# A two-level seven-product matmul on one core: a sixth block product by sevens in every second group, small sums on GpSimd, half of C scaled last

## The chip, the cores and the metric

The kernel runs on one core of a Trainium2 chip. The engines are named as in the profile: PE is TensorE (matmuls), DVE is VectorE, ACT is ScalarE, POOL is GpSimd, SP is SyncE, which here only issues DMAs. The metric is the device time of one execution in microseconds (us).

## The reference

```
cs = np.cumsum(x, axis=1)
diff = cs - np.concatenate([zeros, cs[:, :-1, :]], axis=1)
return np.matmul(diff, w).astype(np.float32)
```

x is 8 x 2048 x 2048 and w is 2048 x 2048, both float32. The difference of the running sum is x itself, so what is computed is x @ w, with x seen as 16384 rows of 2048. The kernel computes just that.

## The kernel before

x is cut into 128 row tiles of 128 rows. The first four are multiplied plainly, the next eight by two shorter forms; they are the head. Then come 29 groups of four tiles, g, h = g + 2, k = g + 1 and l = g + 3. Each row of x is divided by its largest magnitude (`weigh` on ACT, `scale_of` on DVE), narrowed to float16 by ACT (`narrow`), and turned by a DMA transpose (`turn`); the factor that undoes the scaling is made by POOL (`unit_of`, one element for each partition).

Each group is a product of two rows of blocks by w, where w is cut in 2 x 2 blocks B11 to B22 of 1024 x 1024. On the outer level seven block products replace eight (P1 to P7). Their left sides are blocks of x or wide sums of them: S1 = A21 + A22, S2 = S1 - A11, S3 = A11 - A21, S4 = A12 - S2 with g or h as row 1 and k or l as row 2. Their right sides are blocks of w or T1 to T4, made once in the head. P6 is S2 x T2 and P7 is S3 x T3.

On the inner level a block product is itself done by seven (`by_seven` and what stands in `plan`): the two tiles g and h (or k and l) are the two rows, and the block of w is cut in quarters of 512 columns by 512 rows. A product by seven has seven quarter products p1 to p7 of 4 matmuls each, 28; a whole one (`whole`, in four pieces for each tile) has 32. Before, P1 to P5 go by seven, P6 and P7 whole: 5 x 28 + 2 x 32 = 204 matmuls a group. The left sides s1 to s4 of the quarter products are small sums of x on DVE (`small_sums`, `total`, 128 x 512), held in four scratch places. Their right sides Q1 to Q4 are quarters of w or differences of them. Those with no room to stay are made again each time in the one buffer `flow` by a fill (`fill_by`): a step named `P2.fp4` fills flow for the quarter product p4 of P2.

Results gather in eight PSUM banks. ACT takes a bank to a tile of C in SBUF with the row's factor (`keep`), DVE adds a bank times the factor to it (`add`); a `merge` adds a copy back into a bank. A finished 128 x 512 tile of C is stored (`put`), and its buffer, one of seven, is free again.

Each engine works its instructions strictly in the order written. That order is the list `ORDER`: names of steps with the number of groups ahead, run through once for each group. Loads of x go through F, a ring in SBUF: three places for the first half of a tile and two for the second (line 101). The narrowed tile lies in its first half's place until both transposes have read it, so a place comes free with the second transpose.

Of the kernel before, what the change touches and what calls it, by code (L numbers as in the profile page):

```python
# [10 lines left out]
def kernel(  # L11
# [6 lines left out]
    nc = tc.nc  # L18
    P = 128
# [112 lines left out]
    def scale_of(t):  # L132
        if t < END:
            m2 = sums_of.pop(t)
            m, s, u = (m2[:, i : i + 1] for i in (2, 3, 4))
            scales[t], unit[t] = s, u
            after(
                "dve",
                lambda: nc.vector.tensor_scalar(m, m2[:, :1], m2[:, 1:2], TINY, ADD, MAX),  # L139
            )  # L140
            after("dve", lambda: nc.vector.reciprocal(s, m))  # L141
            sizes[t] = m

    def unit_of(t):
        if t < END:
            u, m = unit[t], sizes.pop(t)
            after("pool", lambda: nc.gpsimd.tensor_scalar(u, m, uw, None, MUL))  # L147
# [346 lines left out]
    class Inner:  # L494
# [20 lines left out]
        def weights(self):  # L515
            places = dict(
                p1=self.t11, p2=self.t21, p3=self.t22, p4=self.Q4,
                p5=self.Q1, p6=self.Q2, p7=self.Q3,
            )
            return {j: pieces_of(t) for j, t in places.items()}  # L520
# [22 lines left out]
    def total(dst, p, q, op):  # L543
        after("dve", lambda: nc.vector.tensor_tensor(dst.all, p.all, q.all, op))  # L544
# [388 lines left out]

    def fill_by(op, a, b):
        def some():
            x, y = (in_twos(t) for t in (a, b))
            after("dve", lambda: nc.vector.tensor_tensor(in_twos(flow), x, y, op))  # L937

        return some

    sevens = {
# [8 lines left out]
                "p5": fill_by(SUB, quarter_of(1, 1, 1), quarter_of(6, 1, 0)),  # L950
# [5 lines left out]

    class Group:
        def __init__(self, g):
# [27 lines left out]
        def quarter(self, P, j, b, fresh):  # L986
            inner, passes = sevens[P]
            if j in passes:
                self.step(f"{P}.f{j}", passes[j])

            def some():
                to, a = self.bank(b, fresh), self.sums[P][j]
                quarter(
                    to, self.real(a), passed if j in passes else inner.weights()[j], fresh
                )
                if isinstance(a, str):
                    self.drop(a, scratch)

            self.step(f"{P}.{j}", some)

        def small_sums(self, P, a, b, dead, places=()):
# [5 lines left out]
            def one(j, p, q, op):  # L1007
                if isinstance(to[j], str):
                    self.take(to[j], scratch)
                total(self.real(to[j]), self.real(p), self.real(q), op)  # L1010
# [37 lines left out]

        def row(self, c):
            return self.tiles[c[3] if c[1] == "1" else {"g": "k", "h": "l"}[c[3]]]  # L1050

        def keep(self, c, b, let=False):
            def some():
                keep(self.take(c, free), self.at[b], unit[self.row(c)])
                self.close(b, let)

            self.step(f"keep.{c}", some)

        def add(self, c, b, tag, let=False):
            def some():  # L1060
                add(self.at[c], self.at[b], unit[self.row(c)])
                self.close(b, let)

            self.step(f"add.{c}.{tag}", some)

        def put(self, c):
            n = 2 * (c[2] == "2") + int(c[4])
            self.step(f"put.{c}", lambda: put(self.at.pop(c), self.row(c), n))

        def plan(self):  # L1070
            tiles = self.tiles
            half = {}
            for c, t in tiles.items():
# [3 lines left out]
                self.step(f"scale.{c}", scale_of, t)  # L1077
# [74 lines left out]
            self.whole("P7", T3, half["g"][0], half["h"][0], *x)  # L1152
# [43 lines left out]
    put.C12g1+0 turn1.h+1 add.C12h1.q+0 P4.p6+0 P4.p5+0 P1.cg+1 P1.p2+1  # L1196
    add.C12h0.q+0 put.C12h0+0 P1.s1+1 narrow1.k+1 P4.s4+0 P4.p3+0 turn0.k+1
    keep.C21g1+0 P1.s2+1 P1.s4+1 P1.p5+1 add.C22h0.x+0 P1.ct+1 add.C21h1.e+0
    unit.h+1 P1.p6+1 unit.g+1 add.C21g1.q+0 add.C21g0.x+0 weigh0.l+1 P1.s3+1
    weigh1.l+1 turn1.k+1 P2.cv+1 P4.p4+0 add.C21g1.x+0 put.C12h1+0 put.C21g1+0  # L1200
    P1.m1+1 P4.p7+0 P1.fp4+1 put.C21g0+0 load.g+2 P2.s1+1 P2.s2+1 P1.p7+1
    P1.m2+1 P2.s4+1 P2.p1+1 P1.p3+1 keep.C11g1+1 S1.g+1 S2.g+1 P1.p4+1
    keep.C11g0+1 add.C21h1.q+0 scale.l+1 unit.l+1 narrow0.l+1 put.C22h0+0
    put.C21h1+0 P2.p2+1 add.C11g0.v+1 P6g.0+1 P2.fp4+1 P2.p6+1 turn0.l+1
    narrow1.l+1 turn1.l+1 keep.C11h1+1 P6g.1+1 P2.s3+1 add.C11g1.q+1 unit.k+1
    S4.g+1 P2.p5+1 P6g.3+1 keep.C11h0+1 add.C11h1.e+1 P2.p7+1 keep.C21h0+0
    add.C11h1.q+1 P6g.2+1 weigh0.g+2 load.h+2 add.C21h0.x+0 P5.p1+1 P2.p4+1
    S3.g+1 keep.C12g1+1 P2.p3+1 keep.C12g0+1 add.C11h0.q+1 put.C11h0+1 P5.fp5+1
    weigh1.g+2 S1.h+1 P7g.0+1 P5.s1+1 P7g.1+1 scale.g+2 P5.cg+1 P5.s2+1 P5.s4+1
    put.C21h0+0 narrow0.g+2 narrow1.g+2 S2.h+1 P5.s3+1 P5.p2+1 P5.p5+1 P5.ct+1  # L1210
    add.C11g1.e+1 P5.fp4+1 P5.p6+1 P5.m1+1 put.C11g0+1 keep.C22g0+1 weigh0.h+2
    weigh1.h+2 S4.h+1 P3.s1+1 put.C11h1+1 P6h.2+1 P6h.1+1 put.C11g1+1 P3.s2+1
    P6h.3+1 P6h.0+1 keep.C12h1+1 P5.p7+1 P5.m2+1 keep.C22h1+1 S3.h+1 P3.s4+1
    P3.s3+1 P7g.2+1 P7g.3+1 P5.p4+1 add.C22g0.x+1 P3.fp2+1 P5.p3+1 keep.C12h0+1
    add.C12h1.z+1 P7h.0+1 load.k+2 P3.p2+1 scale.h+2 narrow0.h+2 P3.p1+1 P7h.2+1
    put.C22g0+1 turn0.g+2 turn1.g+2 add.C12g0.z+1 weigh0.k+2 add.C12g0.q+1
    put.C12g0+1 P4.fp4+1 keep.C22g1+1 P7h.1+1 P7h.3+1 add.C22g1.x+1 put.C22g1+1
    P3.p3+1 add.C22h1.x+1 P4.s1+1 P4.s3+1 put.C22h1+1 keep.C22h0+1 P3.p6+1
    P3.p4+1 add.C12g1.q+1 add.C12g1.z+1 turn0.h+2 add.C12h0.z+1 weigh1.k+2
    narrow1.h+2 load.l+2 P3.p5+1 scale.k+2 P4.p2+1 P4.p1+1 keep.C21g0+1  # L1220
    keep.C21h1+1 P3.p7+1 narrow0.k+2 P1.p1+2 add.C12g1.e+1 add.C12h1.e+1 P4.s2+1
# [16 lines left out]
    groups = [Group(g) for g in range(PLAIN + 8, END, 4)]  # L1238
    for c in groups[0].tiles:
        for s in ("load", "weigh0", "weigh1", "scale", "unit", "narrow0", "narrow1", "turn0", "turn1"):  # L1240
            del groups[0].do[f"{s}.{c}"]
    del groups[1].do["load.g"]
    before = {"P1.s4": lambda: less(*(half_of(t, 0) for t in (in_1.Q2, in_1.t22, in_1.Q1))), "P5.s3": in_5.third}
    for b in range(-early, len(groups) - late):
        for name, ahead in ORDER:
            i = b + ahead
# [39 lines left out]
```

## Time and profile before

| | |
|---|---|
| median of 3 runs | 1456.42 us (1456.38 to 1456.72) |
| profiled execution, first to last instruction | 1455.0 us (no other time is given for it) |
| granted TensorE clock, mean | 0.999 |
| PE / DVE / ACT / POOL busy | 1441.1 / 1333.3 / 967.5 / 48.6 us |
| DMA | 351.59 MB, mean 242 GB/s |

A row of instruction groups reads: line, engine, operation, out <- in, shapes, count, then busy us and mean ns of one, then the engine's idle time before them and who ended it. A row of the windows reads: the stretch in us, its length, then busy us and number of instructions for PE, PE's weight loads, DVE, ACT and POOL, then clock, DMA share and GB/s. A row of the waits reads: who waited for whom, us in total, times, longest. A row of the order of time reads: start, length, engine, line, operation.

### The profile page before, as it was taken

The numbers are of one execution on the slowest core, as the hardware profiler recorded it, in microseconds if no ns is written. First come the engines' busy times: TensorE is split into PE (matmuls) and PEld (weight loads), VectorE is DVE, ScalarE is ACT, GpSimd is POOL, SyncE is SP. The second block draws the span as 40 slices with busy tenths as digits, with TensorE's granted clock in tenths as the row PEclk, the third lists the DMA queues.
The fourth block names the chain that finished last, engine by engine and source line by source line (L and its number), as shares of the span: only waits on it lengthen the run. The fifth ranks groups of instructions, "written<-read, shape, count | busy, mean of one in ns | idle before, by whom it ended". The sixth has DMA issues, their size and how long they took to land.

```text
span 1455.0 us, 20120 instructions
## 1 busy us (share of the span) xinstructions
PE 1441.1 (99%) x6673; PEld 652.6 (45%) x6679; DVE 1333.3 (92%) x2302; ACT 967.5 (66%) x1446; POOL 48.6 (3%) x136
## 2 busy tenths in 40 slices
PE   8999999999999999999999999999999999999998
PEld 3444444444444444444444444444444444444443
DVE  7998899999999999999999999999999999999998
ACT  5887656676666666667666667766666766666662
POOL 0111000000000000000000000000000000000000
PEclk9999999999999999999999999999999999999999
DMA  9999868898888998878998888998878898888983
GB/s 360 367 240 299 236 171 234 248 246 232 234 237 237 248 253 230 235 236 233 260 241 233 231 228 240 260 238 241 225 235 247 247 233 239 226 244 246 253 203 123
DMA packets 377752, 351.59 MB, mean 242 GB/s; under 512 B 274800, under 2 KB 274800, under 8 KB 377520
## 3 DMA queue, kind: packets, MB, share of 16 engines
q1 hardware_dynamic: 377088, 348.47, 84.9%
q0 software_dynamic: 560, 1.84, 0.3%
q8 instruction: 52, 0.85, 0.2%
q14 instruction: 52, 0.43, 0.1%
HBM read 150.99 MB, written 134.22 MB: 196 GB/s over the span
## 4 chain that ended last, share of the span: by engine, by line
PE 96%; DMA 2%; DVE 1%; issue 0%; ACT 0%; SPq 0%; DVEq 0%; ACTq 0%
PE b L573 61%; PE b L554 32%; PE b L275 2%; DMA W<-in_w_dram 1%; DMA W<-in_x_dram 1%; DVE c L584 1%; ACT wb L259 0%; PE b L400 0%; DVE x L544 0%; SPq L219 0%; DVE b L1030 0%; DVE flow L937 0%; DVE inner L544 0%; DVE W L541 0%; ACT c L581 0%
## 5 line engine op out<-in xcount | busy, mean ns | idle before, releaser
L584 DVE SCALAR_TENSOR_TENSOR c<-b,of,c 128x512 f32<-128x512 f32 x790 | 574.1, 747 | 74.3 <-PE b L573 64.3
L554 PE MATMUL b<-W,x 128*128 128x512 f16 x2144 | 506.6, 379 | 0.0
L581 ACT ACTIVATE c<-b,of 128x512 f32<-128x512 f32 x492 | 312.6, 680 | 230.9 <-PE b L573 113.3
L573 PE MATMUL b<-W,x 128*128 128x512 f16 x1892 | 452.4, 379 | 0.8 <-ACT b L1023 0.7
L158 ACT ACTIVATE F<-F,of 128x1024 f16<-128x1024 f32 x246 | 282.2, 1147 | 174.8 <-DVE of L141 172.6
L573 PEld LDWEIGHTS <-x 128*128 128x128 f16 x2488 | 243.4, 98 | 295.3 <-issue 2.7
L554 PEld LDWEIGHTS <-x 128*128 128x128 f16 x2144 | 209.8, 98 | 253.0 <-DVE x L544 0.2
L123 ACT ACTIVATE waste<-F 128x1024 uint8<-128x1024 f32 x246 | 259.3, 1054 | 4.6 <-DMA F<-in_x_dram 2.5
L573 PEld LDWEIGHTS <-inner 128*128 128x128 f16 x1648 | 161.2, 98 | 195.6 <-issue 1.3
L573 PE MATMUL b<-W,inner 128*128 128x512 f16 x944 | 242.2, 379 | 0.9 <-DVE b L1030 0.9
L544 DVE TENSOR_TENSOR x<-x,x 128x1024 f16<-128x1024 f16 (+1 forms) x388 | 226.6, 584 | 3.3
L573 PE MATMUL b<-flow,x 128*128 128x512 f16 x588 | 150.9, 379 | 0.0
L573 PE MATMUL b<-inner 128*128 128x512 f16 x472 | 121.1, 379 | 0.0
L937 DVE TENSOR_TENSOR flow<-W 128x2048 f16<-128x2048 f16 x87 | 105.8, 1216 | 0.0
L1030 DVE TENSOR_TENSOR b<-b,c 128x512 f32<-128x512 f32 x116 | 80.6, 695 | 13.9 <-PE b L573 13.9
L147 POOL TENSOR_SCALAR of<-of,uw 128x1 f32<-128x1 f32 x124 | 43.6, 370 | 1306.7 <-DVE of L139 704.1
L937 DVE TENSOR_TENSOR flow<-W,inner 128x2048 f16<-128x2048 f16 x58 | 70.8, 1220 | 0.0
L1023 ACT COPY c<-b 128x512 f32<-128x512 f32 x58 | 33.4, 576 | 51.3 <-PE b L573 51.3
L275 PE MATMUL b<-wb,xP 128*128 128x512 bf16 x234 | 57.0, 395 | 5.3 <-ACT wb L259 3.9
L544 DVE TENSOR_TENSOR inner<-x 128x512 f16<-128x512 f16 x117 | 49.4, 422 | 2.9 <-DMA x<-F 0.9
L1023 ACT COPY b<-b 128x512 f32<-128x512 f32 x87 | 51.2, 588 | 0.5 <-PE b L573 0.5
L544 DVE TENSOR_TENSOR inner<-x,inner 128x512 f16<-128x512 f16 x117 | 49.2, 421 | 2.0
(67 smaller groups left out, 530.0 us busy)
## 6 DMA issues: line engine op xcount, KB each, us to landing
F<-in_x_dram SPq DMA_DIRECT2D x246, 512.0 KB, 5.1
out_dram<-c SPq DMA_DIRECT2D x492, 256.0 KB, 3.0
W<-in_w_dram SPq DMA_DIRECT2D x32, 512.0 KB, 9.6
W<-in_x_dram SPq DMA_DIRECT2D x16, 256.0 KB, 7.2
x<-F SPq DMA_TRANSPOSE x246, 3.4
out_dram<-o POOLq DMA_DIRECT2D x5, 256.0 KB, 4.1
out_dram<-o SPq DMA_DIRECT2D x5, 256.0 KB, 3.5
xP<-in_x_dram SPq DMA_DIRECT2D x1, 1024.0 KB, 5.1
```

What stands on the lines that cost most here:

```text
L123: lambda: nc.scalar.activation(waste, where[t][i], ABS, scale=1.0 / ROW, accum_out=sums_of[t][:, i : i + 1],),
L147: after("pool", lambda: nc.gpsimd.tensor_scalar(u, m, uw, None, MUL))
L158: lambda: nc.scalar.activation(narrowed(t)[:, ds(i * NH, NH)], where[t][i], COPY, scale=s),
L275: lambda: nc.tensor.matmul(ps[r][n], xP[:, r, ko, :], wb[h, ko][:, ds(n * NB, NB)], start=(ko == 0), stop=(ko == KO - 1),),
L544: after("dve", lambda: nc.vector.tensor_tensor(dst.all, p.all, q.all, op))
L554: said = nc.tensor.matmul(to[n], a[k], b[k][:, n, :], start=(first and k == 0), stop=(k == KH - 1), skip_group_check=True,)
L573: said = nc.tensor.matmul(to, a[k], b[k], start=(first and k == 0), stop=(k == 3), skip_group_check=True)
L581: after("act", lambda: nc.scalar.activation(c, p, COPY, scale=u))
L584: after("dve", lambda: nc.vector.scalar_tensor_tensor(c, p, u, c, MUL, ADD))
L937: after("dve", lambda: nc.vector.tensor_tensor(in_twos(flow), x, y, op))
L1023: after("act", lambda: nc.scalar.copy(c, p))
L1030: after("dve", lambda: nc.vector.tensor_tensor(t, p, s, ADD))
```

## The change

One round of the new `ORDER` covers a pair of groups; `0:` and `1:` name the first and second of it, and every second group has the mark `more`.

- In a group with `more`, P7 goes by seven (`onto`): 28 matmuls for 32. Its results go onto the banks in which P6 lies. It needs four small sums, four fills of flow (two of them made from what lies in flow), four copies of a bank by ACT (c1, c5, c6, c7) and six merges (a1, a5g, a5h, a6, a7h, a7k).
- P5's Q1 stays in SBUF, in the place F[:, 2, :]; its fill before p5 falls away in all groups. The ring of x has two places for both halves from the twelfth tile of the queue on.
- Eleven small sums of one group of a pair and ten of the other go to POOL (`ON_POOL`).
- Eight of a group's sixteen tiles of C (`LATE`) are gathered without the factor: ACT copies, DVE adds bank and tile with no multiplication, and one more ACT instruction (`last`) scales the tile before it is stored. The last group is left as it was.
- The size of a row and its reciprocal are two steps, `scale` and `recip`.

```diff
+    THREE = 11
     for i, t in enumerate(queue_of_x):
-        where[t] = [F[:, i % 3, :], F[:, 3 + i % 2, :]]
+        j = i % 3 if i < THREE else (i - THREE) % 2
+        where[t] = [F[:, j, :], F[:, 3 + i % 2, :]]
...
-    def total(dst, p, q, op):
-        after("dve", lambda: nc.vector.tensor_tensor(dst.all, p.all, q.all, op))
+    ON_POOL = """
+    0:P1.s1 0:P1.s3 0:P1.s4 0:P2.s1 0:P2.s2 0:P2.s3 0:P2.s4 0:P3.s2 0:P4.s3 0:P5.s4
+    1:P2.s1 1:P2.s2 1:P2.s3 1:P2.s4 1:P3.s1 1:P3.s2 1:P3.s4 1:P4.s2 1:P4.s3 1:P4.s4
+    1:P5.s4
+    """.split()
+
+    def total(dst, p, q, op, pool=False):
+        if pool:
+            after("pool", lambda: nc.gpsimd.tensor_tensor(dst.all, p.all, q.all, op))
+        else:
+            after("dve", lambda: nc.vector.tensor_tensor(dst.all, p.all, q.all, op))
...
+    in_5.Q1 = F[:, 2, :].bitcast(f16).rearrange("p (k n) -> p k n", k=4)
...
+    in_7 = Inner(5, None, None, None)
...
                 "p4": fill_by(SUB, quarter_of(1, 1, 0), quarter_of(6, 1, 0)),
-                "p5": fill_by(SUB, quarter_of(1, 1, 1), quarter_of(6, 1, 0)),
+            },
+        ),
+        "P7": (
+            in_7,
+            {
+                "p5": fill_by(SUB, in_7.t12, in_7.t11),
+                "p6": fill_by(SUB, in_7.t22, flow),
+                "p4": fill_by(SUB, in_7.t21, flow),
+                "p7": fill_by(SUB, in_7.t22, in_7.t12),
             },
...
+    LATE = 'C12g0 C12g1 C12h1 C12h0 C11g1 C11h1 C21g1 C21h1'.split()
...
+            self.late = LATE if g + 4 < END else ()
...
+        def onto(self, P, h0, h1, g0, g1):
+            q, e = f"{P}q", f"{P}e"
...
+                    after("act", lambda: nc.scalar.copy(c, p))
...
+            self.quarter(P, "p1", q, True)
+            self.step(f"{P}.c1", snap(f"{P}1", q))
+            self.merge(f"{P}.a1", g0, g0, f"{P}1", let=True)
+            self.quarter(P, "p2", g0, False)
+            self.quarter(P, "p5", e, True)
+            self.step(f"{P}.c5", snap(f"{P}5", e, True))
+            self.merge(f"{P}.a5g", g1, g1, f"{P}5")
+            self.merge(f"{P}.a5h", h1, h1, f"{P}5", let=True)
+            self.quarter(P, "p3", g1, False)
+            self.quarter(P, "p6", q, False)
+            self.step(f"{P}.c6", snap(f"{P}6", q))
+            self.merge(f"{P}.a6", g1, g1, f"{P}6", let=True)
+            self.quarter(P, "p7", q, False)
+            self.step(f"{P}.c7", snap(f"{P}7", q, True))
+            self.merge(f"{P}.a7h", h1, h1, f"{P}7")
+            self.merge(f"{P}.a7k", h0, h0, f"{P}7", let=True)
+            self.quarter(P, "p4", h0, False)
...
+                if c in self.late:
+                    after("dve", lambda: nc.vector.tensor_tensor(to, p, to, ADD))
+                else:
+                    add(to, p, u)
...
+            if c in self.late:
+                self.step(f"last.{c}", lambda: keep(self.at[c], self.at[c], unit[self.row(c)]))
...
-            self.whole("P7", T3, half["g"][0], half["h"][0], *x)
+            if self.more:
+                self.small_sums("P7", A("g", 0), A("h", 0), True)
+                self.onto("P7", *x)
+            else:
+                self.whole("P7", T3, half["g"][0], half["h"][0], *x)
...
-    put.C12g1+0 turn1.h+1 add.C12h1.q+0 P4.p6+0 P4.p5+0 P1.cg+1 P1.p2+1
...
+    0:add.C12g0.q+1 1:unit.g+1 0:P3.s4+1 0:add.C12g0.z+1 0:P5.m1+1 0:P6h.3+1 0:P3.p6+1
```

What stands in a row now, at three places. First DVE, from the fill before P3's p2 on. Here b are PSUM banks, c tiles of C and copies, x the turned tiles, inner the scratch places; L937 (L957 after) is a fill, L1030 (L1063) a merge, L544 (L561) a sum of x. Before:

```order
L937 TENSOR_TENSOR flow<-W,inner 128x2048
L584 SCALAR_TENSOR_TENSOR c_759<-b_789,of,c_759 128x512
L139 TENSOR_SCALAR of<-of 128x1
L141 RECIPROCAL of<-of 128x1
L584 SCALAR_TENSOR_TENSOR c_767<-b_785,of,c_767 128x512
L584 SCALAR_TENSOR_TENSOR c_767<-b_789,of,c_767 128x512
L937 TENSOR_TENSOR flow<-W 128x2048
```

and after, in a group with P7 by seven, from the small sum s2 of P7 on:

```order
L561 TENSOR_TENSOR inner<-inner,x_63 128x512
L150 RECIPROCAL of<-of 128x1
L957 TENSOR_TENSOR flow<-W,flow 128x2048
L1063 TENSOR_TENSOR b_790<-b_786,c_755 128x512
L601 SCALAR_TENSOR_TENSOR c_763<-b_788,of,c_763 128x512
L561 TENSOR_TENSOR inner<-x_63,inner 128x512
L1063 TENSOR_TENSOR b_791<-b_791,c_771 128x512
L1063 TENSOR_TENSOR b_787<-b_786,c_755 128x512
L1129 TENSOR_TENSOR c_751<-b_787,c_751 128x512
L1063 TENSOR_TENSOR b_791<-b_791,c_747 128x512
L957 TENSOR_TENSOR flow<-W,flow 128x2048
```

Two new fills that read flow itself stand between merges, and an addition without a factor (L1129) among them. Second, POOL's whole order from the head's stores on, before:

```order
L285 DMA out_dram<-o_120 128x512
L285 DMA out_dram<-o_124 128x512
L147 ISA
L147 TENSOR_SCALAR of<-of,uw 128x1 x124
L1281 UNCONDITIONAL_BRANCH
```

and after, a stretch of one pair:

```order
L155 TENSOR_SCALAR of<-of,uw 128x1 x3
L559 TENSOR_TENSOR inner<-x_66 128x512
L155 TENSOR_SCALAR of<-of,uw 128x1
L559 TENSOR_TENSOR x_70<-x_68,x_70 128x512
L559 TENSOR_TENSOR inner<-inner,x_64 128x512
L559 TENSOR_TENSOR inner<-x_64,inner 128x512
L155 TENSOR_SCALAR of<-of,uw 128x1
L559 TENSOR_TENSOR inner<-x_64,x_66 128x512
L559 TENSOR_TENSOR inner<-x_66 128x512
L559 TENSOR_TENSOR inner<-x_67,inner 128x512
```

POOL had the rows' factors alone; now the sums of x stand between them. Third, the DMAs that SP issues around a load of x, before:

```order
L111 DMA F<-in_x_dram 128x1024 x2
L595 DMA out_dram<-c_747 128x512
L595 DMA out_dram<-c_755 128x512
L171 DMA_TRANSPOSE x_69<-F 128x8x128
L171 DMA_TRANSPOSE x_70<-F 128x8x128
L111 DMA F<-in_x_dram 128x1024 x2
```

and after:

```order
L179 DMA_TRANSPOSE x_69<-F 128x8x128
L612 DMA out_dram<-c_771 128x512
L179 DMA_TRANSPOSE x_70<-F 128x8x128
L612 DMA out_dram<-c_747 128x512
L113 DMA F<-in_x_dram 128x1024 x4
L612 DMA out_dram<-c_767 128x512
```

The loads of two tiles now stand together, behind the transposes of the tiles whose places they take.

More of the change, by code (lines that the diff above doesn't have):

```diff
@@ L519, in weights @@
             )
-            return {j: pieces_of(t) for j, t in places.items()}
+            return {j: pieces_of(t) for j, t in places.items() if t is not None}
     passed = [flow[:, k, :] for k in range(4)]
@@ L1053, in some @@
             def some():
-                keep(self.take(c, free), self.at[b], unit[self.row(c)])
+                to, p, u = self.take(c, free), self.at[b], unit[self.row(c)]
+                if c in self.late:
+                    after("act", lambda: nc.scalar.copy(to, p))
+                else:
+                    keep(to, p, u)
                 self.close(b, let)
@@ L1203 @@
[L1203 to L1221, printed above, removed]
+    0:add.C12g0.q+1 1:unit.g+1 0:P3.s4+1 0:add.C12g0.z+1 0:P5.m1+1 0:P6h.3+1 0:P3.p6+1
+    1:turn0.g+1 0:last.C12g0+1 0:P5.p7+1 1:weigh1.h+1 0:P5.fp4+1 1:turn1.g+1
@@ new lines @@
+    1:P1.p6+1 1:load.l+1 1:turn0.k+1 1:narrow1.k+1 1:P1.s3+1 1:turn1.k+1 1:P1.m1+1
+    1:weigh0.l+1 0:add.C21g0.x+1 0:P4.p3+1 1:P1.p2+1 0:add.C21g1.x+1 1:P1.p7+1 1:P2.p1+1
+    0:add.C21g1.q+1 1:P1.p3+1 0:last.C12h1+1 0:put.C21g0+1 1:P2.s2+1 1:P2.cv+1
+    1:weigh1.l+1 0:P4.p7+1 0:put.C12h1+1 0:put.C12g1+1 1:keep.C11g0+1 1:P1.m2+1
+    1:scale.l+1 1:recip.l+1 1:narrow0.l+1 1:turn0.l+1 1:S1.g+1 1:keep.C11g1+1 1:P2.s4+1
+    1:narrow1.l+1 0:last.C21g1+1 1:P2.p2+1 1:add.C11g0.v+1 1:put.C11g0+1 1:P2.p6+1
@@ L1222 @@
+    0:keep.C11h0+2 1:last.C21g1+1 1:load.h+2 0:keep.C22g0+2 1:weigh0.g+2 0:P3.p2+2
+    1:weigh1.g+2 1:put.C21g1+1 0:P5.s1+2 0:P5.s2+2 0:P5.s4+2 0:add.C11h0.q+2 0:P3.s1+2
+    0:P6h.0+2 1:scale.g+2 0:put.C11h0+2 0:P7g.1+2 0:P7g.0+2 0:put.C11h1+2 0:P5.p6+2
+    0:P5.p5+2 0:P6h.1+2 0:P3.s3+2 0:P3.s2+2 1:recip.g+2 1:narrow0.g+2 1:narrow1.g+2
+    0:P5.s3+2 0:P5.ct+2 0:last.C11g1+2 0:P6h.2+2
     """
```

111 lines of the change are left out of this document (89 added, 22 removed).

## The prediction

> **What bounds the kernel now.** I read the page's busy shares and slices first, then the chain that ended last, the busy time of each engine over five whole groups, and the waits of PE and DVE from 150 us on.
>
> ```profile
> PE 1441.1 (99%) x6673; PEld 652.6 (45%) x6679; DVE 1333.3 (92%) x2302; ACT 967.5 (66%) x1446; POOL 48.6 (3%) x136
> ...
> PE   8999999999999999999999999999999999999998
> ...
> DVE  7998899999999999999999999999999999999998
> ACT  5887656676666666667666667766666766666662
> POOL 0111000000000000000000000000000000000000
> PEclk9999999999999999999999999999999999999999
> ```
> ```profile
> 206.22 18.13 PE b L573 x84
> 250.25 18.13 PE b L573 x84
> ```
> ```profile
> 206.22:250.25 44.03, 44.03 (x205) 19.98 (x204) 40.81 (x73) 29.86 (x46) 1.07 (x4) 1.00 0.89 239
> ...
> 382.33:426.36 44.03, 44.03 (x206) 19.97 (x204) 40.78 (x72) 29.61 (x46) 1.07 (x4) 1.00 0.88 240
> sum 220.14, PE 220.14 PEld 99.81 DVE 203.93 ACT 148.29 POOL 5.34; mean PE 44.03 PEld 19.96 DVE 40.79 ACT 29.66 POOL 1.07
> ```
> ```profile
> PE b L573 <- DVE b L1030: 0.9, 1, 0.9
> PE b L573 <- ACT b L1023: 0.7, 1, 0.7
> ```
> ```profile
> DVE c L584 <- PE b L573: 59.8, 141, 1.1
> DVE b L1030 <- PE b L573: 13.3, 28, 0.5
> ```
>
> PE is the bound: 99% busy at full clock, and from 150 us on it waits twice, 1.6 us in all. The chain repeats at 206.22 and 250.25: one group of four row tiles takes 44.03 us. Eighty-four matmuls of 128x512 take 18.13 us, so one costs 18.13 / 84 = 0.2158 us, and 204 of them make 44.03 us: the group is its matmuls and nothing else. The columns of the windows are stretch, length, then PE, PEld, DVE, ACT, POOL: DVE is busy 40.79 us of a group, ACT 29.66, POOL 1.07. DVE's waits are for PE. A saved matmul is therefore worth 0.2158 us as long as DVE, the next engine, does not fall behind.
>
> **The change, part by part.** Prices come from these groups (busy us, mean ns of one):
>
> ```profile
> L584 DVE SCALAR_TENSOR_TENSOR c<-b,of,c 128x512 f32<-128x512 f32 x790 | 574.1, 747 | 74.3 <-PE b L573 64.3 <-ACT c L581 1.3
> L581 ACT ACTIVATE c<-b,of 128x512 f32<-128x512 f32 x492 | 312.6, 680 | 230.9 <-PE b L573 113.3 <-issue 63.2 <-PE b L554 28.6
> L158 ACT ACTIVATE F<-F,of 128x1024 f16<-128x1024 f32 x246 | 282.2, 1147 | 174.8 <-DVE of L141 172.6
> L123 ACT ACTIVATE waste<-F 128x1024 uint8<-128x1024 f32 x246 | 259.3, 1054 | 4.6 <-DMA F<-in_x_dram 2.5
> L544 DVE TENSOR_TENSOR x<-x,x 128x1024 f16<-128x1024 f16 x240 | 164.4, 685 | 1.2
> L937 DVE TENSOR_TENSOR flow<-W 128x2048 f16<-128x2048 f16 x87 | 105.8, 1216 | 0.0
> L1030 DVE TENSOR_TENSOR b<-b,c 128x512 f32<-128x512 f32 x116 | 80.6, 695 | 13.9 <-PE b L573 13.9
> L544 DVE TENSOR_TENSOR inner<-x 128x512 f16<-128x512 f16 x117 | 49.4, 422 | 2.9 <-DMA x<-F 0.9
> L1023 ACT COPY c<-b 128x512 f32<-128x512 f32 x58 | 33.4, 576 | 51.3 <-PE b L573 51.3
> ```
>
> PE. P7 of an odd group is seven quarters of 4 matmuls instead of 32: 4 matmuls less. There are 29 groups after the head, 14 of them odd: 14 x 4 x 0.2158 = 12.1 us. An even group keeps its 204. A pair is now 404 x 0.2158 = 87.18 us of PE.
>
> DVE, per pair, from 2 x 40.79 = 81.58 us. The fill for P5's p5 goes in both groups, because that difference now has a place of its own in F: -2 x 1.216 = -2.43. The 21 small sums leave for POOL: -21 x 0.422 = -8.86. The late tiles of C (eight of sixteen) get 18 additions a group without the scale; the nearest row is the merge, 695 for 747 ns: -36 x 0.052 = -1.87. P7 in the odd group brings four fills (+4.86), four small sums (+1.69) and six merges (+4.17). Sum 79.14 us, 91% of 87.18; before it was 93% of 44.03. So DVE has 8.0 us spare a pair instead of 6.5. Without POOL's share it would be 88.0 us, more than PE.
>
> ACT, per pair, from 59.32: sixteen last scalings +16 x 0.680 = +10.88, sixteen plain copies for scaled ones -16 x 0.104 = -1.66, four copies in P7 +2.30; 70.8 us, 81%. Hidden, but c1, c5, c6 and c7 of P7 now stand in a fuller queue, and merges on DVE wait for them. If ACT were late by 0.6 us there, P7's p2 and p3 would be the late ones; I leave a part of the stall below for it. Splitting the reciprocal from the size costs nothing: same two instructions.
>
> SP: each tile's load now waits for the transposes of the tile two before it, not three.
>
> ```profile
> F<-in_x_dram SPq DMA_DIRECT2D x246, 512.0 KB, 5.1
> out_dram<-c SPq DMA_DIRECT2D x492, 256.0 KB, 3.0
> ...
> x<-F SPq DMA_TRANSPOSE x246, 3.4
> ```
> ```profile
> 722.67 0.91 SPq L111 DMA_DIRECT2D F<-in_x_dram  x2
> ...
> 731.86 1.04 ACT L123 ACTIVATE waste<-F 128x1024 uint8<-128x1024 f32 x1
> ...
> 734.04 1.05 ACT L123 ACTIVATE waste<-F 128x1024 uint8<-128x1024 f32 x1
> ...
> 740.95 1.15 ACT L158 ACTIVATE F<-F,of 128x1024 f16<-128x1024 f32 x1
> ...
> 743.28 4.02 SPq L171 DMA_TRANSPOSE x<-F  x2
> ```
>
> Eight tiles a pair and two slots: a slot has 87.18 / 4 = 21.8 us for a tile. The bare chain is load 5.1, two weighings 2.1, two narrowings 2.3 and the transposes: the pair of them takes 4.0 us to issue and the second lands about 2.1 us after that (3.4, less the 1.3 that its own issue takes); 15.6 us, 6.2 less than there is. Before, the third tile of a group held its slot from 722.67 to about 749.4, 26.7 us of the 33.0 that three slots gave, but its load went out 9.2 us ahead of its weighing, 4.1 more than the 5.1 it needs: 22.6 us. So the new order must close 0.8 us; most of the 22.6 is waiting between weighing and narrowing (735 to 741 us), and in the new order only one other row of ACT stands there for that tile. Price 0; the other end is rival two. The stores of late tiles go after the last scaling, and a buffer c comes back 3.0 us after its store; I cost that at nothing, covered by ACT's 16 us idle a pair.
>
> POOL. No row shows POOL at 512 elements. From below, the same sum on DVE, 0.42 us; from above, the longest POOL row of this trace, 1.89 us:
>
> ```profile
> 165.67 1.89 POOL L147 TENSOR_SCALAR of<-of,uw 128x1 f32<-128x1 f32 x1 [11.22 <-DVE of L139]
> 165.69 1.21 DVE L541 TENSOR_TENSOR W<-W 128x2048 f16<-128x2048 f16 x1
> ...
> 166.81 0.69 DVE L541 TENSOR_TENSOR S<-W 128x1024 f16<-128x1024 f16 x1
> ...
> 167.42 0.74 DVE L584 SCALAR_TENSOR_TENSOR c<-b,of,c 128x512 f32<-128x512 f32 x1
> ```
> ```profile
> 202.55 0.54 POOL L147 TENSOR_SCALAR of<-of,uw 128x1 f32<-128x1 f32 x2 [34.99 <-DVE of L139]
> ```
>
> I take the middle, 1.16 us: 21 x 1.16 = 24 us, 28% of a pair. By the Trainium skill's page "GPSIMD Engine Reference", section 3.1, such an addition runs at about 2.6 cycles an element; 512 at 1.2 GHz would be an estimate of 1.1 us, and the sum would not change.
>
> The rows show more: one element on POOL takes 0.27 us at 202 us, and 1.89 us at 165.67, where DVE began an operation on two SBUF inputs 0.02 us later; it ended only at 167.56, after both such operations (167.50) and under the first one that reads PSUM. So the two engines do exclude each other. Whether a POOL sum holds DVE up likewise is not shown, since POOL's operation is too short. The Trainium skill, "SBUF — State Buffer", section "Who interferes with whom", says so: a DVE instruction with two SBUF inputs and a GpSimd instruction that reads SBUF take a common port for their whole length, and the second one blocks; the trace agrees for POOL behind DVE.
>
> What it costs: DVE's operations on two SBUF inputs are 16 wide sums (0.685), 23 small ones and 14 fills a pair, 37.7 us. The other 41.4 us of DVE and its 8.0 idle are open to POOL. A sum begins under an operation on PSUM of about 0.7 us, so some 0.45 us of it stick out, and about every second time an SBUF operation comes next: 0.22 us x 21 = 4.7 us, less than the 8.0 spare. On average nothing reaches PE. From both ends: 0, or 21 whole sums, 24.4 us, 16.4 more than is spare.
>
> Averages hide places. A fill must fall between two matmul quarters that both read flow. The tightest of them before:
>
> ```profile
> 727.50 1.03 PE L573 MATMUL b<-flow,x 128*128 128x512 f16 x4
> ...
> 728.57 1.23 DVE L937 TENSOR_TENSOR flow<-W,inner 128x2048 f16<-128x2048 f16 x1
> ...
> 730.09 0.38 PE L573 MATMUL b<-flow,x 128*128 128x512 f16 x1
> ```
>
> The fill starts 0.04 us after the last reader's end (728.53), ends at 729.80, and PE reads at 730.09, 0.29 us spare with two quarters between. An odd group now has three gaps with just two quarters between readers (p5 to p6 and p4 to p7 of P7, P7's p7 to P5's p4). One POOL sum in front of such a fill costs 1.16 - 0.29 = 0.87 us, as much as the four matmuls save (0.86). At the first gap POOL's P5.s4 and the fill are released by the same quarter; in the rows above DVE went first in such a race, so I take that as free. The other sums nearby (P3.s2, P3.s4, P4.s2) follow under merges and additions. I allow 0.2 us of stall per odd group for these places and ACT's copies: 14 x 0.2 = 2.8.
>
> Sum against the profiled execution: 1455.0 - 12.1 + 2.8 = 1445.7 us of span; the median of the runs, 1456.4, lies 1.4 above that span, so 1447.
>
> **The rivals.** One, slower: POOL's sums block the fills. For it: the exclusion in the rows, and the three gaps with 0.29 us. Against it: 8 us spare, and POOL mostly runs beside additions. It decides from one blocked fill per odd group on, which gives 1456.4 - 12.1 + 14 x 0.87 = 1456.5; with all three, 14 x 2.61 = 36.5, it is 1480.8. This is what the skill's rule on the port would make of it.
>
> Two, slower: with two slots the loads come late; ACT stands at the weighing, DVE at the size behind it, and additions behind that. It decides from a slot time of 21.8 us on. If it stays at the 22.6 of before, a group takes two slot times, 45.2 us, 1.6 more than the new 43.59: 29 x 1.6 = 46.4 against 12.1, 1490.7. Against it: 6 us of room over the bare chain.
>
> Three, no change: stalls of 0.66 to 1.07 us per odd group eat the gain, 1453.5 to 1459.3.
>
> **How the numbers follow.** PE stays the bound with small stalls: 0.55, own range 1444 to 1453.5. No change, within 0.2% (2.9 us, about what runs of this kernel can tell): 0.08. POOL against DVE: 0.25. Late loads: 0.12. So faster 0.55, same 0.08, slower 0.37. Low end: all of 12.1 with no stall is 1444.3; I put 1443.5 for the tail. High end: the three blocked fills with a little of the late loads, 1484; about 0.12 lies above.
>
> **What would show it.** Right: per pair 87.2 us with 404 matmuls, PE's waits below 3 us, DVE near 79 us a pair, POOL's sums near 1.2 us each. Wrong: PE waiting for DVE at flow's readers, fills longer than 1.22 us or sums of x on DVE longer than 0.42 and 0.69 where POOL overlaps, or ACT waiting for F's loads.

## The result: 3.5% slower

| | before | after |
|---|---|---|
| median of the runs | 1456.57 us (1456.38 to 1457.01) | 1507.83 us (1506.53 to 1508.71) |
| profiled execution, span | 1455.0 us | 1505.6 us |
| PE / DVE / ACT / POOL busy | 1441.1 / 1333.3 / 967.5 / 48.6 us | 1446.9 / 1321.8 / 1115.9 / 460.9 us |

The ratio is 1.0351, 95% interval 1.0336 to 1.0365. The forecast was 1447.0 us and the range ended at 1484. Against the 1444.3 us that the matmuls alone would take by the prediction's sum, 63.5 us are lost.

The page of the changed kernel, busy shares and slices:

```profile
PE 1446.9 (96%) x6617; PEld 644.1 (43%) x6623; DVE 1321.8 (88%) x2166; ACT 1115.9 (74%) x1726; POOL 460.9 (31%) x440
...
PE   8999999999999999999999999999999999999998
...
DVE  7998889888898888989889898888988889898897
```

The 56 matmuls are gone (6673 to 6617), the instructions of DVE (2302 to 2166) and POOL (136 to 440) moved as the change has it, and the slices still read 9 for PE everywhere: 4 us lost in 92 do not show in a scale of tenths. The windows show them. These are the first and the last of five successive pairs of groups, and their mean (columns as before: stretch, length, PE, PE's weight loads, DVE, ACT, POOL):

```profile
360.40:452.18 91.78, 88.52 (x406) 39.38 (x404) 80.49 (x136) 70.05 (x110) 29.80 (x31) 1.00 0.85 229
...
727.04:818.55 91.51, 88.47 (x405) 39.38 (x404) 80.99 (x136) 69.81 (x110) 30.89 (x31) 1.00 0.85 230
sum 458.15, PE 442.04 PEld 196.63 DVE 403.69 ACT 349.20 POOL 153.09; mean PE 88.41 PEld 39.33 DVE 80.74 ACT 69.84 POOL 30.62
```

A pair takes 458.15 / 5 = 91.6 us where 87.2 was forecast, at full clock. Neither DVE (80.7 us busy) nor ACT (69.8) is full. So the loss is in waits, and the waits from 150 to 1440 us say which:

```profile
DVE c L1129 <- ACT c L1118: 37.1, 28, 2.3
...
ACT waste L125 <- DMA F<-in_x_dram: 32.4, 33, 3.2
...
PE b L590 <- DVE b L1063: 26.8, 20, 1.9
PEld L590 <- DVE inner L561: 22.2, 16, 1.8
...
PE b L590 <- DVE c L1129: 8.6, 15, 0.7
```

In the kernel before, the wait of the same additions for ACT was

```profile
DVE c L584 <- ACT c L581: 0.6, 1, 0.6
```

L1118 is ACT's copy of a bank to a late tile of C, L1129 DVE's addition to such a tile, L1063 a merge into a bank, L561 a sum of x. PE waits for merges and sums, DVE for ACT's copies. Counted by the starts of the matmuls and named by the written order, in 12 whole pairs, PE loses about 4.5 us a pair between matmuls, at few places: 1.75 us ahead of P1's p7 in the second group of a pair, 0.75 ahead of P3's p1 there, 0.2 to 1.3 ahead of P5's p7 of the first group in 5 of the 12 pairs, 0.2 to 0.4 on average at five others.

The groups of instructions show DVE's operations on two SBUF inputs longer than before, some of them by more than twice:

```profile
L957 DVE TENSOR_TENSOR flow<-W 128x2048 f16<-128x2048 f16 x86 | 113.1, 1315 | 0.0
...
L561 DVE TENSOR_TENSOR inner<-x 128x512 f16<-128x512 f16 x73 | 41.9, 574 | 3.4 <-DMA x<-F 2.4
...
L561 DVE TENSOR_TENSOR inner<-x,x 128x512 f16<-128x512 f16 x16 | 16.3, 1017 | 0.0
```

The worst place, P1's p7 of a second group, in order of time (start, length, engine, line):

```profile
671.76 0.57 ACT L1118 COPY c<-b 128x512 f32<-128x512 f32 x1
...
672.23 0.69 ACT L598 ACTIVATE c<-b,of 128x512 f32<-128x512 f32 x1
...
672.81 0.60 ACT L1056 COPY b<-b 128x512 f32<-128x512 f32 x1
673.32 0.72 ACT L598 ACTIVATE c<-c,of 128x512 f32<-128x512 f32 x1
...
673.94 0.58 ACT L1056 COPY c<-b 128x512 f32<-128x512 f32 x1
674.41 0.60 ACT L1118 COPY c<-b 128x512 f32<-128x512 f32 x1
...
675.04 0.69 DVE L1129 TENSOR_TENSOR c<-b,c 128x512 f32<-128x512 f32 x1 [2.04 <-ACT c L1118]
...
675.65 1.22 DVE L957 TENSOR_TENSOR flow<-W,S 128x2048 f16<-128x2048 f16 x1
675.69 2.19 POOL L559 TENSOR_TENSOR inner<-inner,x 128x512 f16<-128x512 f16 x1 [3.43 <-PE b L590]
...
676.78 1.38 DVE L561 TENSOR_TENSOR inner<-x,x 128x512 f16<-128x512 f16 x1
...
678.08 0.69 DVE L1063 TENSOR_TENSOR b<-b,c 128x512 f32<-128x512 f32 x1
...
678.82 1.02 PE L590 MATMUL b<-W,inner 128*128 128x512 f16 x4 [1.54 <-DVE b L1063]
```

Read it from the end. PE's p7 waits for the merge P1.m1 (678.08). The merge stands on DVE behind the small sum P1.s3 (676.78), which takes 1.38 us instead of 0.42. P1.s3 stands behind the fill (675.65), and that behind the addition add.C21h1.e (675.04), ahead of which DVE sat idle for 2.04 us. It waited for ACT's copy keep.C21g1 (674.41 to 675.01): both read one PSUM bank, and the second reader began only when the first was done. The bank itself had been ready at about 671.2, when its last matmul ended. The copy came late because of what ACT has ahead of it in its order: a row without a break from 671.76 on, with the new last scaling at 673.32 and P1.ct at 673.94, which cannot start before PE's P1.p5 (ended 673.83). So the last scaling itself costs at most 0.11 us here; what puts the copy late is its place behind P1.ct. In the order before, keep.C21g1 stood ahead of P1.ct. The second half of the delay is POOL: its sum P2.s2 is released at 675.69, 0.04 us after DVE's fill began, and ends only at 677.88, 1.01 us after the fill's end (an undisturbed sum takes 1.16). Meanwhile P1.s3 on DVE is held, until 678.16.

### The profile page after: what moved, and what is told of

Same layout as the page of the kernel before. It is cut to its first block, busy times and chain, and to the rows that moved or that the text cites. A ratio compares the mean times of both kernels' runs of the same rounds, so it can differ in the third digit from the quotient of the medians.

```text
span 1505.6 us, 20953 instructions
## 1 busy us (share of the span) xinstructions
PE 1446.9 (96%) x6617; PEld 644.1 (43%) x6623; DVE 1321.8 (88%) x2166; ACT 1115.9 (74%) x1726; POOL 460.9 (31%) x440
## 5 line engine op out<-in xcount | busy, mean ns | idle before, releaser
L590 PE MATMUL b<-W,x 128*128 128x512 f16 x2004 | 485.8, 379 | 14.6 <-DVE c L1129 8.9
L571 PE MATMUL b<-W,x 128*128 128x512 f16 x1696 | 393.5, 379 | 0.1
L1129 DVE TENSOR_TENSOR c<-b,c 128x512 f32<-128x512 f32 x504 | 337.5, 683 | 60.4 <-ACT c L1118 37.6
L125 ACT ACTIVATE waste<-F 128x1024 uint8<-128x1024 f32 x246 | 259.5, 1055 | 37.1 <-DMA F<-in_x_dram 35.6
L598 ACT ACTIVATE c<-b,of 128x512 f32<-128x512 f32 x268 | 178.3, 684 | 133.4 <-PE b L590 59.4
L601 DVE SCALAR_TENSOR_TENSOR c<-b,of,c 128x512 f32<-128x512 f32 x286 | 208.4, 744 | 24.9 <-ACT c L598 11.0
L561 DVE TENSOR_TENSOR x<-x,x 128x1024 f16<-128x1024 f16 (+1 forms) x345 | 208.4, 612 | 20.4 <-PE b L571 14.7
L559 POOL TENSOR_TENSOR inner<-x,inner 128x512 f16<-128x512 f16 x87 | 115.4, 1327 | 335.9 <-DVE inner L561 230.9
L598 ACT ACTIVATE c<-c,of 128x512 f32<-128x512 f32 x224 | 158.6, 721 | 18.9 <-DVE c L1129 18.9
L1118 ACT COPY c<-b 128x512 f32<-128x512 f32 x224 | 127.6, 583 | 39.7 <-PE b L571 20.3
L559 POOL TENSOR_TENSOR inner<-x 128x512 f16<-128x512 f16 x58 | 76.6, 1320 | 261.0 <-DVE x L561 145.3
L1063 DVE TENSOR_TENSOR b<-b,c 128x512 f32<-128x512 f32 x200 | 137.1, 693 | 17.0 <-ACT c L1056 14.3
L957 DVE TENSOR_TENSOR flow<-W 128x2048 f16<-128x2048 f16 x86 | 113.1, 1315 | 0.0
L559 POOL TENSOR_TENSOR inner<-inner,x 128x512 f16<-128x512 f16 x58 | 77.8, 1341 | 75.8 <-PE b L590 58.8
```

The lines of the kernel that those rows point to most:

```text
L125: lambda: nc.scalar.activation(waste, where[t][i], ABS, scale=1.0 / ROW, accum_out=sums_of[t][:, i : i + 1],),
L559: after("pool", lambda: nc.gpsimd.tensor_tensor(dst.all, p.all, q.all, op))
L571: said = nc.tensor.matmul(to[n], a[k], b[k][:, n, :], start=(first and k == 0), stop=(k == KH - 1), skip_group_check=True,)
L590: said = nc.tensor.matmul(to, a[k], b[k], start=(first and k == 0), stop=(k == 3), skip_group_check=True)
L598: after("act", lambda: nc.scalar.activation(c, p, COPY, scale=u))
L601: after("dve", lambda: nc.vector.scalar_tensor_tensor(c, p, u, c, MUL, ADD))
```

## Experiments

Every time is a median, beside 1456.6 to 1456.8 for the kernel before, timed along with each of them, and 1507.8 for the changed one, which was timed once.

**POOL's sums left out.**

```diff
         if pool:
-            after("pool", lambda: nc.gpsimd.tensor_tensor(dst.all, p.all, q.all, op))
+            pass
```

> The changed kernel without the 21 small sums a pair that GpSimd makes: neither GpSimd nor DVE makes them, the quarter products read what lies in the scratch places. Theory A (GpSimd's sums and DVE's operations on two SBUF inputs exclude each other, and PE waits for the DVE work that is held up): PE's stalls of 4.5 us a pair go almost wholly, 1444 to 1453. Rival B (the stalls come from the two-place ring of x, from ACT's fuller queue or from the scarce buffers c): they stay, above 1490.

Measured: 1482.38 us, ratio 1.0175 [1.016, 1.019]. Groups and waits:

```profile
L957 DVE TENSOR_TENSOR flow<-W 128x2048 f16<-128x2048 f16 x86 | 104.6, 1216 | 0.0
...
L561 DVE TENSOR_TENSOR inner<-x 128x512 f16<-128x512 f16 x73 | 30.6, 419 | 2.9 <-DMA x<-F 1.9
```
```profile
DVE c L1129 <- ACT c L1118: 39.8, 29, 2.8
```

Neither theory holds. Fills and sums are back at 1.216 and 0.42 us, so it is POOL that lengthens them, and 25 us go with its sums. The other 38 us, down to 1444.3, are not POOL's: DVE's wait for ACT's copies is still there.

**All sums on DVE.** `ON_POOL` is left empty.

> The changed kernel with all small sums on DVE, in the same order. Theory A: no exclusion any more, but DVE has 88.0 us of work a pair for 87.2 of PE and its waits for PE on top; 89 to 91 us a pair, 1470 to 1500, still below the changed kernel's 1508. Rival C (GpSimd's help is worth more than the exclusion costs): slower than 1508.

Measured: 1533.80 us, ratio 1.0531 [1.0514, 1.0549]; DVE 1382.8 us busy. Sums on POOL cost 25 us more than sums made nowhere, but 26 us less than sums on DVE. Handing them to POOL was right in itself; the price was not zero.

**Is it late results or a held DVE?** POOL makes its sums in four pieces of 128 columns into a place that nobody reads.

```diff
-            after("pool", lambda: nc.gpsimd.tensor_tensor(dst.all, p.all, q.all, op))
+            for i in range(4):
+                x, y = (a.all[:, ds(i * NB // 4, NB // 4)] for a in (p, q))
+                after("pool", lambda: nc.gpsimd.tensor_tensor(idle, x, y, op))
```

> The changed kernel in which each of GpSimd's sums is made in four pieces of 128 columns into a place that nobody reads: the same inputs read at about the same times, but neither PE nor DVE waits for a result; the quarter products read what lies in the scratch places. If the cost is DVE being held up at the port (theory A), 1480 or more. If it is the results coming late (rival D), 1460 or less. Pieces may let DVE in between them, which would put it in the middle.

Measured: 1524.83 us, ratio 1.0468 [1.0453, 1.0484]. Nobody waits for a sum, and it is slower still. But the run does not separate the two theories. The four pieces keep POOL busy longer (508 to 593 ns each in the groups, some 2.2 us for a sum of 1.16), and now others wait for POOL: ACT for the rows' factors, which POOL makes behind the pieces, and DVE until POOL has read a tile of x.

```profile
ACT c L601 <- POOL of L155: 19.3, 17, 1.8
DVE x L564 <- POOL idle L562: 17.5, 27, 3.9
```

One such place is a new stall of PE of about 1.1 us in nearly every pair, some 15 us in all, while the whole kernel is 17.0 us slower than the changed one:

```profile
271.02 0.69 ACT L601 ACTIVATE c<-b,of 128x512 f32<-128x512 f32 x1 [1.28 <-POOL of L155]
...
271.76 1.02 PE L593 MATMUL b<-inner 128*128 128x512 f16 x4 [0.95 <-ACT c L601]
```

That late results are the lesser part, the changed kernel's own waits show:

```profile
DVE inner L561 <- POOL inner L559: 7.5, 11, 1.0
ACT c L598 <- POOL of L155: 3.5, 6, 0.9
PEld L590 <- POOL inner L559: 0.7, 2, 0.4
```

**The same in the kernel before.** There every group gets 40 differences of 128 x 128 on POOL into a place that nobody reads; all other work is kept.

```diff
+            if t >= PLAIN + 12:
+                for i in range(EXTRA[t % 4]):
+                    x, y = (blocks[:, 0, 0, i % 8, j, : NB // 4] for j in range(2))
+                    after("pool", lambda: nc.gpsimd.tensor_tensor(idle, x, y, SUB))
```

> The kernel before, unchanged in its result, with GpSimd given sums that nobody waits for: behind each of its scale factors 8 or 12 sums of two fixed pieces of w (128 x 128, four of them as large as one small sum of x), 40 a group. If GpSimd's reads and DVE's operations on two SBUF inputs exclude each other (theory A), DVE, with 3.2 us idle in 44.03, loses more than it has spare in some groups, and PE waits: 1465 to 1500. If GpSimd runs beside DVE at no cost (rival E), 1456 to 1458.

Measured: 1472.86 us, ratio 1.0113 [1.0096, 1.0130].

```profile
PE 1452.1 (99%) x6679; PEld 647.3 (44%) x6679; DVE 1383.4 (94%) x2302; ACT 968.3 (66%) x1446; POOL 650.9 (44%) x1256
```
```profile
PEld L560 <- DVE x L550: 16.7, 56, 0.4
...
PEld L579 <- DVE inner L550: 12.8, 28, 0.5
```

DVE is 50 us longer at its unchanged work (1333.3 to 1383.4), and PE's weight loads, which had waited 0.4 us for sums of x before, now wait 29.5. Nobody waits for these results, and the waits there have no row in which an engine waits for POOL. The exclusion alone costs 16 us in a kernel that has nothing else of the change.

**Shorter loads.** Each tile's load brings a quarter of the columns from the third group on.

```diff
-                    where[t][i], x2[ds(t * P, P), ds(i * NH, NH)]
+                    where[t][i][:, :NH // 4] if t >= PLAIN + 12 else where[t][i],
+                    x2[ds(t * P, P), ds(i * NH, NH // 4 if t >= PLAIN + 12 else NH)],
```

> The changed kernel with each load of x from the third group after the head on cut to a quarter of its columns, so that it lands sooner and the DMA engines have less to move; the products are of stale columns. Theory A: no loss comes from the ring, 1500 to 1510. Rival B (loads come late): 1470 or less. The trace of the changed kernel has ACT waiting 32.4 us for loads of x, so a few us of gain are possible under A too.

Measured: 1501.30 us, ratio 1.0306 [1.0291, 1.0322]. ACT's wait for F falls from 32.4 to

```profile
ACT waste L126 <- DMA F<-in_x_dram: 3.0, 5, 0.8
```

and the stalls ahead of P5's p7 go with it. The late loads of the ring are real, but worth 6.5 us here.

**The order of two readers.** DVE's addition to C21h1 is put ahead of ACT's copy of C21g1 from the same bank, in both groups of a pair and in the last group (where the copy to C21h1 moves up with it); nothing else moves.

```diff
-            self.keep("C21g1", e)
-            self.add("C21h1", e, "e", let=True)
+            self.keep("C21g1", e, let=True)
+            self.add("C21h1", e, "e")
...
-    0:P4.s3+1 1:P1.ct+1 0:keep.C21g1+1 0:add.C21h1.e+1 1:P1.fp4+1 0:put.C22h1+1
+    0:P4.s3+1 1:P1.ct+1 0:add.C21h1.e+1 0:keep.C21g1+1 1:P1.fp4+1 0:put.C22h1+1
```

> The changed kernel with one swap: the addition of the quarter bank to C21h1 (DVE) stands ahead of the copy of the same bank to C21g1 (ACT), so DVE no longer waits for that copy, which is late behind the copy for P1's merge. Theory F (a second reader of a PSUM bank waits for the first one, and so DVE waits for a late ACT): PE's stall of 1.75 us at P1's p7 in the second group of a pair falls to 0.8 or less, 14 x 0.95 = 13 us: 1490 to 1497. Rival (the stall at p7 is GpSimd's sum alone, which holds DVE's sum): 1505 or more.

Measured: 1482.47 us, ratio 1.0174 [1.0159, 1.0189]: 25 us from one swap, about twice what was expected. The wait of additions for copies, 37.1 us, is now

```profile
DVE c L1129 <- ACT c L1118: 5.1, 16, 0.3
```

and P1's p7 starts without a stall in all 12 pairs: the whole 1.75 us a pair goes. POOL's share of it goes too: P1.s3, no longer late, is done before POOL's sum begins, and its row reads 418 ns where it read 1017.

```profile
L561 DVE TENSOR_TENSOR inner<-x,x 128x512 f16<-128x512 f16 x16 | 6.7, 418 | 0.0
```

With all work kept, this and the second reordering below are the fastest variants that were tried; both stay behind the kernel before.

**With two of the sums back on DVE** (P1.s1 of the first and P4.s2 of the second group), on top of the swap.

> The same swap, and two of the 21 sums back on DVE: P1.s1 of the first group (PE waits 0.42 us for it at P1's p5) and P4.s2 of the second (it holds the fill before P7's p4, 0.38 us of stall). Theory A: 14 x 0.8 = 11 us less than with the swap alone, 1480 to 1487. If DVE's 0.84 us more a pair outweigh it: the same or more than with the swap alone.

Measured: 1483.89 us, ratio 1.0188 [1.0172, 1.0203]; no gain, the expectation was missed. The fills of L957 from flow go from 1389 to 1214 ns, but PE now waits 6.8 us for small sums on DVE (L561): DVE is held less by POOL, but has more to do itself.

**No second reader at three places.** The copies of C21g1 (both groups) and of C22h1 (second group) read their own SBUF tile instead of the bank.

```diff
                 if c in self.late:
+                    if c == "C21g1":
+                        p = to
                     after("act", lambda: nc.scalar.copy(to, p))
+                elif c == "C22h1" and self.more:
+                    keep(to, to, u)
```

> The changed kernel in which three of ACT's instructions a pair read the SBUF tile they write in place of the PSUM bank: the copies to C21g1 and, in the second group of a pair, the one to C22h1, so those tiles hold nothing useful. ACT does as much, but DVE's additions from the same banks no longer wait for it. Theory F: the stall before P3's p1 (0.75 us) goes, and that at P1's p7 (1.75) falls to 0.8: 14 x 1.7 = 24 us less than the changed kernel, 1480 to 1488. Rival B (ACT, the ring, the buffers c): 1500 or more.

Measured: 1470.39 us, ratio 1.0099 [1.0084, 1.0114]: 37.4 us less. The stalls at P1's p7 and P3's p1 are gone, some 1.8 us a pair remain. The edit removes a little more than the wait of a second reader: the three copies no longer wait for the matmuls that fill the bank either.

**That, and no sums on POOL.**

> The three copies that read their own tile instead of the bank, as in the run before, and POOL's 21 sums left out as well (nobody makes them, so the products that read them are wrong). Alone the first took 37.4 us off 1507.8, the second 25.4. If the second readers of a bank and the exclusion between POOL and DVE are two causes with places of their own, both together take off about 60 us: 1447 to 1455, the 1444.3 that the matmuls need and what the late loads leave, up to 6.5. Rival: the two meet in the same stalls and are counted twice, then 1458 to 1470 remains and something that neither touches holds PE for 14 us or more.

Measured: 1458.94 us, ratio 1.0017 [1.0007, 1.0026]. This is the rival's case: the two causes meet in the same stalls. Alone they take off 25.4 and 37.4 us, together 48.9. But 14.6 us stay above the 1444.3 of the matmuls, spread over places that stall in at most 5 of 12 pairs.

**That, and half loads.** The load's columns are `NH // 2` from the third group on.

> The run before this (own tile for three copies, no sums on POOL, 1458.9) with half of the columns of x loaded for each tile from the third group on, so that a slot's load is about half as long (the rest of the slot keeps what an older tile left there). In that run ACT still waited 33 us for the loads of F between 150 and 1440 us, and PE's remaining stalls, about 14 us, stood in only 2 to 5 of 12 pairs each. If the late loads are the third cause: 1444 to 1450, ACT's waits for F below 10 us. Rival: within 2 us of 1458.9; then the rest is DVE's own order.

Measured: 1446.61 us, ratio 0.9929 [0.9913, 0.9946]. Page, and the first and last of five pairs in the windows:

```profile
PE 1430.4 (99%) x6617; PEld 644.9 (45%) x6623; DVE 1284.1 (89%) x2166; ACT 1113.8 (77%) x1726; POOL 73.0 (5%) x136
```
```profile
351.14:438.43 87.29, 87.29 (x406) 39.39 (x405) 78.39 (x136) 69.71 (x110) 4.74 (x8) 1.00 0.76 193
...
700.45:787.69 87.24, 87.24 (x405) 39.44 (x404) 78.27 (x136) 69.62 (x110) 3.24 (x8) 1.00 0.75 193
```

PE fills the pair: 87.3 us of 87.3. ACT's wait for F fell only from 32.9 to 18.4 us, not below 10 as expected; what is left of it no longer reaches PE. Whether the ring's two places or the traffic of the loads is the reason isn't told apart, since both are halved.

**A second reordering.** On top of the swap, at P3's p1 of the second group: DVE merges P7.a6 ahead of the addition to C12h1, and PE makes P7's p3 ahead of P3's p1.

```diff
-    1:P3.s2+1 1:P3.s4+1 0:weigh1.h+2 1:add.C12h1.z+1 1:P7.a6+1 1:keep.C12h0+1
-    1:keep.C22g1+1 1:P3.p1+1 0:turn0.g+2 1:P7.fp4+1 1:add.C12g0.q+1 0:scale.h+2
-    0:turn1.g+2 1:last.C12g0+1 1:put.C12g0+1 1:P7.p3+1 1:add.C22g1.x+1 1:P7.p4+1
+    1:P3.s2+1 1:P3.s4+1 0:weigh1.h+2 1:P7.a6+1 1:add.C12h1.z+1 1:keep.C12h0+1
+    1:keep.C22g1+1 1:P7.p3+1 1:P3.p1+1 0:turn0.g+2 1:P7.fp4+1 1:add.C12g0.q+1 0:scale.h+2
+    0:turn1.g+2 1:last.C12g0+1 1:put.C12g0+1 1:add.C22g1.x+1 1:P7.p4+1
```

> The kernel with the addition to C21h1 ahead of the copy of C21g1 (1482.5), all work kept, and at the second place, P3's p1 of the second group, two moves: DVE makes the merge P7.a6 while ACT copies C22h1, ahead of the addition to C12h1, and PE makes P7's p3 before P3's p1, which needs the bank that this addition frees. The stall there was 0.75 to 0.80 us per pair, with 14 pairs 10 to 11 us. If the chain from P5's p7 through two readers of one bank is what holds it: 1471 to 1476, and P3's p1 without a stall. Rival: the chain only hands on its wait (to P7's p3 behind the merge, or to the addition to C12g0): 1480 or more.

Measured: 1480.94 us, ratio 1.0168 [1.0153, 1.0183]. This is the rival's case: P3's p1 no longer stalls, and the wait went on to the fill behind the addition on DVE, which now meets a sum on POOL (1690 ns for 1389 with the swap alone). PE's P7.p4 now stalls 1.1 us in every pair but one, and 0.8 there:

```profile
L957 DVE TENSOR_TENSOR flow<-W,flow 128x2048 f16<-128x2048 f16 x28 | 47.3, 1690 | 0.0
```
```profile
PE b L590 <- DVE flow L957: 14.7, 18, 1.0
```

**The late scaling alone, in the kernel before.** Eight tiles a group are gathered without the factor; the last scaling stands right ahead of the store.

```diff
+            if c in self.late:
+                def some():
+                    keep(self.at[c], self.at[c], unit[self.row(c)])
+                    put(self.at.pop(c), self.row(c), n)
+                self.step(f"put.{c}", some)
+                return
```

> The kernel before with one part of the change alone: eight tiles of C a group are copied and added without the scale and scaled by ACT right ahead of their store. No sum goes to POOL, P7 stays 32 matmuls, the ring keeps three slots, the order is that of before. ACT gets 8 x 0.680 - 8 x 0.104 = 4.6 us a group more, 29.7 to 34.3 of 44.03; DVE saves 18 x 0.05 = 0.9. If ACT's fuller queue by itself makes the second readers of a bank late: 1460 to 1475, with DVE's additions waiting for ACT's copies for 10 us or more between 150 and 1440 us. Rival: 1455 to 1458, ACT's 9.7 idle us a group cover it in before's order, and the lateness comes from where the new order of a pair puts the copies.

Measured: 1531.09 us, ratio 1.0508 [1.0492, 1.0523], far outside both theories. In order of time, one stall:

```profile
715.55 0.69 ACT L581 ACTIVATE c<-b,of 128x512 f32<-128x512 f32 x1 [1.39 <-DMA out_dram<-c]
...
717.04 0.59 ACT L1059 COPY c<-b 128x512 f32<-128x512 f32 x1 [0.81 <-DMA out_dram<-c]
...
717.68 1.02 PE L554 MATMUL b<-W,x 128*128 128x512 f16 x4 [1.85 <-ACT c L1059]
```

A tile's buffer leaves after the last scaling and so comes back later from its store; ACT's next copy of a bank waits for a buffer, and the bank's next matmul waits for the copy. ACT waits 72 us for stores between 150 and 1440 us there, 0.9 in the kernel before. The sign that the first theory named is there as well: DVE's additions wait 34.2 us for ACT's plain copies. But ACT is late here because of the buffers, so the run does not show whether its fuller queue alone would do it. In the changed kernel ACT's plain copies wait 8.6, 2.2 and 0.5 us for stores: its order of a pair avoids most of this cost. How much of the lateness in the changed kernel is the last scalings' was not measured; at P1's p7 the rows above leave them at most 0.11 us.

## Why the prediction was wrong

Taken away one after the other, the causes make this row:

| | us | step |
|---|---|---|
| changed kernel | 1507.83 | |
| three second readers of a bank gone | 1470.39 | -37.4 |
| and POOL's sums gone | 1458.94 | -11.5 |
| and loads halved | 1446.61 | -12.3 |
| matmuls alone, by the prediction | 1444.3 | -2.3 |

The steps depend on the order: taken first, POOL's sums are 25.4 (and the second readers then 23.4) and the loads, at a quarter, 6.5.

- **PE's saving: right.** 56 matmuls went, and a pair takes 87.3 us once nothing holds it, 87.18 forecast.
- **DVE's and ACT's sums: nearly right.** DVE 78.3 us a pair undisturbed for 79.14, 80.7 with the exclusion; ACT 69.8 for 70.8.
- **ACT costed at nothing ("hidden"): the step that failed first.** The prediction named c1, c5, c6 and c7 of P7 as the copies that may come late, left part of 0.2 us per odd group for them, and priced only the sum of ACT's work. What came late was keep.C21g1, a copy with a second reader behind it: 2.04 us of DVE idle and, with POOL's sum on top, 1.75 of PE a pair; the copy of C22h1, with a second reader too, adds the 0.75 ahead of P3's p1. Before, the same two readers of C21g1's bank stood in the same order, with 0.6 us of wait in the whole run. ACT at 76% has room on average, but the new order puts this copy behind P1.ct, which waits for PE. The swap alone gives back 25 us. That the place behind P1.ct is the reason is read from the rows; a run with only that copy moved back ahead of P1.ct was not made.
- **POOL's sums at 1.16 us: right, with some luck.** The prediction took the middle of two far bounds, 0.42 and 1.89 us. Undisturbed the sums take 1.15 to 1.16; the estimate of 1.1 us from the Trainium skill, "GPSIMD Engine Reference", section 3.1, is 0.06 short.
- **The exclusion costs PE nothing: failed.** The amount was not too small: 4.7 us of DVE a pair were allowed, and DVE is 1321.8 us busy with the sums and 1280.8 without, 41.0 us or 2.8 a pair (14 pairs and a half). The step from there to PE failed: "less than the 8.0 spare, on average nothing reaches PE". The spare time lies elsewhere than the held operations, and 11.5 to 25 us of the kernel's time went with POOL's sums. That DVE is held as POOL is, which the prediction had only from the Trainium skill ("SBUF — State Buffer", "Who interferes with whom"), these runs show.
- **The three tight gaps: mostly right.** PE's matmuls wait 3.0 us for fills in the whole stretch, its weight loads 9.9; at none of the three gaps does PE stall regularly. Of flow's readers only P7's p4 (0.4 us a pair) and P4's p4 (0.2) do, and neither stands behind one of these gaps. The race at the first gap went as told: the fill at 608.76 took 1.20 us, POOL's P5.s4 at 608.91 took 2.08. The 2.8 us allowed in all were meant for the wrong places.
- **The ring at nothing: failed by little.** Rival two's mechanism is there: ACT waits 32.4 us for F, where the kernel before shows no such wait from 150 us on. It is worth 6.5 to 12.3 us and not 46, and the runs that test it move less data as well as shorten the loads, so the ring's share of that stays open.
- **Rival one** had POOL's mechanism, at fills only. The range's high end of 1484 joined it to part of rival two, and left out the second readers, which were the largest part.

## What to carry to other kernels

An engine with a quarter of its time free can still be the one that is waited for: before costing added work at nothing, go through the places where another engine waits for that engine's single instruction (two readers of one bank above all) and look at what stands directly ahead of it in the new order. Where two engines exclude each other, the sum of the overlaps against the spare time says little; look at which held operation has a reader with less slack than one hold. When several stalls remain, take the causes away together as well as singly: singly they gave 25.4, 37.4 and 6.5 us, together 61.2, and the fix that only moved a wait (to 14.7 us at a fill) gained 1.5 us.

## What the runs showed of the hardware

The exclusion between POOL and DVE goes both ways and lasts a whole operation. In order of time, in the changed kernel:

```profile
633.57 1.16 POOL L559 TENSOR_TENSOR inner<-inner,x 128x512 f16<-128x512 f16 x1
633.85 1.96 DVE L957 TENSOR_TENSOR flow<-W,S 128x2048 f16<-128x2048 f16 x1
...
634.82 2.00 POOL L559 TENSOR_TENSOR inner<-x,inner 128x512 f16<-128x512 f16 x1
```

The fill, 1.22 us undisturbed, starts 0.28 us into POOL's sum and takes 1.96: it ends at 635.81, 1.08 after the sum's end at 634.73. POOL's next sum then waits for the fill and ends at 636.82, 1.01 behind it. On DVE's additions that read PSUM no such lengthening shows: 683 ns (L1129) beside POOL's 460.9 us, 684 where POOL makes no sums.

Cutting a POOL sum in four made it longer, not gentler. 128 columns took 0.51 to 0.59 us on average, with holds; undisturbed, in the kernel before with POOL's extra sums, it was

```profile
699.78 0.43 POOL L152 TENSOR_TENSOR idle<-W 128x128 f16<-128x128 f16 x1
```

so four of them take 1.7 us where one of 512 columns takes 1.16. That two engines which only read one PSUM bank come one behind the other was not in the prediction's prices at all, and it was the dearest single cause here; the trace shows the wait and that it goes when the copy reads something else, not whether the chip would need it.
